# RWKV's sample step and first-half head norm placed ahead of the second half of the chunks, with nine buffers for cached keys and values

## The chip, the core and the metric

The kernel runs on one core of a Trainium2 chip. The metric is the device time of one execution in microseconds (us); lower is better. The names used for the engines are those of the profile: PE is the matrix engine (TensorE), PEld its weight loads, DVE the vector engine, ACT the scalar engine, POOL the GpSimd engine, SP the engine that issues most transfers.

## The reference, cut to what matters

One inference step of a two-layer hybrid decoder, for a prompt of 256 tokens and 8 sample rows (one token each) that share the weights. Each layer computes

```
proj = rmsnorm(x) @ w_in                       # one projection for four mixers
ya = moba_attend(q, k, v)                      # prompt: 256 own tokens
                                               # sample: top 3 of 8 cached blocks of 256 tokens, and the own token
yb = rglru_mixer(...)                          # convolution, gates, linear scan
yc = ssd_mixer(...)                            # prompt: 2 chunks of 128; sample: one recurrent step
yd = rwkv_mixer(...)                           # prompt: 256 steps; sample: one step
x = x + concat(ya, yb, yc, yd) @ w_out
x = x + cross_attn(rmsnorm(x), memory)
x = x + peer_ffn(rmsnorm(x))                   # product-key experts
```

In `rwkv_mixer`, y is the output of a recurrence over the tokens. It is normalised head by head (mean and variance over 64 columns), a bonus term sum(r*k*r_k)*v is added, and the sum is multiplied by a gate g. `k_past` and `v_past` of the sample rows are gathered from paged pools by a page table.

## The kernel before, in words

All activations lie feature-major: 128 partitions, then eight blocks of 128 features, then 264 columns (256 prompt tokens and 8 sample rows). A matmul against a float32 weight is made of three float32r matmuls: `load_w` splits a weight tile w into a rounded part wh (ACT) and the rest wl (DVE), and `proj` accumulates wh*hh, wh*hl and wl*hh over eight blocks, 24 matmuls into one PSUM tile `mm`. `inp(c, ...)` is such a projection with chunk c of w_in.

The program is one straight line of instructions. A scheduler puts each engine's instructions in an order from the order in which the source emits them, from their dependencies, from a modelled timeline and from the tiles that pools have free; so the place of a call in the source shifts the order on every engine without fixing it. Instructions of an engine, and the transfers that SP and POOL issue, go strictly in that order. `together()` keeps a group of matmuls adjacent.

The mixer part of a layer (`layer`, from line 464) goes in this order of emission:

- `moba_qk`: four projections and the rotation. Then the small `dt` product.
- `rwkv` is a generator and `next(rw)` runs it to its next `yield`. Its first piece makes seven projections, mixes each token with the one before, and forms decay, gate and the normalised key (a matmul `kn` for each of two head pairs). Its second piece is `rounds(0)`: two `unit`s (one for each head pair) go through the first 128 tokens as two chunks of 64. A unit makes scaled copies (`abd`, `kbd`), products `ob` and `m0`, then five rounds of `xl` and `xm` that invert a triangular matrix by doubling, with DVE's COPY_PREDICATED between them, and then `ob`, `ok`, `z` products, with the state `sl` at the end.
- `moba_sample`: for 8 rows, 16 groups of key pages. A group is four tiles `kvp` of [128, 2, 256], two loaded by SP (line 1221, two transfers of 128 KB each) and two gathered by POOL (line 1225, two indirect transfers each), and eight matmuls `asc` that read all four. So 16 groups need 64 gathers by POOL. After the scores come the selection of the blocks (`a2`, `a3` tiles) and 24 gathered value tiles `kvp` (line 1333), four to a group, with four matmuls `apv` each. All `kvp` tiles share `KVB` = 7 buffers; two more of them are taken by `ptm`, the probabilities, while values are gathered.
- `lru`: four projections and a scan. `ssd`: six projections, the convolution (`xb`), the step sizes (`dz`, `spd`), the decay products `rp`, the chunk products `fs`, `sc`, `y`, then the sample row's step (`t8s`, `sss`, `y16s`, a product `bk` from `bks`) and the norm (`yq`, `gm`, `sn`). Its large scratch tiles `sc1`, `sc2` have the tags `hh` and `hl`.
- `moba_prompt`: scores `as`, a softmax in `asm`, transposes `tp`, products `y`. `asm` and `apt` have the same tags `hh` and `hl`, so they take the buffers of `ssd`'s scratch when that is done.
- three more pieces of `rw`: `rounds(2)`, the two units for the last 128 tokens, which keep scratch in the weight pool's buffers (`unw`, `unwh`, `unwl`, `unz`); then the sample step `rwkv_sample` (`srt`, `srw`, DVE work on [128, 512], a product `bk` from `bkr`), the bonus and `finish(slice(0, 128))`, the head norm of the first 128 tokens; then `finish(slice(128, 264))`.
- products `mk` of the memory tokens, and the split of `ymix`; cross-attention (`w_out` first) follows.

`expand` lays out the sample step's operands through a tile `t8`, whose tag it shares with two tiles of `rwkv` (`up`, `pm`) in a pool with one buffer for that tag. `use(tag)` chooses the PSUM pool that the products in its block take.

Of the kernel before, what the change touches and what calls it, by code (L numbers as in the profile page):

```python
# [224 lines left out]
F32, F32R, F16, I32, U32, U8 = (getattr(mybir.dt, n) for n in ('float32', 'float32r', 'float16', 'int32', 'uint32', 'uint8'))  # L225
# [1 line left out]
OP = mybir.AluOpType  # L227
AX = mybir.AxisListType
EPS = 1e-6
KVB = 7  # L230
NF = 4
XT = 12
GS = 16384.0
# [10 lines left out]
def emit(tc, A, O, layers=(0, 1)):  # L244
# [223 lines left out]
    def layer(l, mx, v, following):  # L468
        me, mp, cm, vc, st = mx.es, mx.mp, mx.cm, mx.vc, mx.st
        st_h = st[:, 0:16].rearrange("p (c b) -> p c b", c=2)  # L470
        st_lc = st[:, 16:64].rearrange("p (c j b) -> p c j b", c=2, j=3)
        st_sc = st[:, 64:160].rearrange("p (c j b) -> p c j b", c=4, j=3)
        st_rs = st[:, 160:216].rearrange("p (c b) -> p c b", c=7)
        hp = me.enter_context(tc.tile_pool(name="h%d" % l, bufs=1, reuse_waits="tile"))
        eh = two(hp, ("eh", "el"), ("hh", "hl"))
        r = rstd(mp, v)
        for c in range(8):
            early(eh, vc('norm_mix'), c)
        if mx.pre is None:
            mx.prepare()  # L480
        pre = mx.pre
        win = A['w_in'][l]

        def inp(c, dst, half=False):

            o = proj(win[c], eh)
            if half:
                stt(dst, o, 0.5, r, OP.mult, OP.mult)
            else:
                tt(dst, o, r, OP.mult)  # L490
        with tc.tile_pool(name="z%d" % l, bufs=1, reuse_waits="tile") as zp:
            q, k = moba_qk(l, mp, cm, load_consts(zp, 'z'), inp)
        ymix = mp.tile([128, 8, NT], F32, name="ymix")

        rs = ExitStack()
        rp_ = rs.enter_context(tc.tile_pool(name="r%d" % l, bufs=1, reuse_waits="tile"))
        sp_ = rs.enter_context(tc.tile_pool(name="s%d" % l, bufs=1, reuse_waits="tile"))
        o = ps([4, NT], "dt")
        for c in range(8):
            for i, (a, b) in enumerate(((mx.dth, eh[0]), (mx.dth, eh[1]), (mx.dtl, eh[0]))):  # L500
                mm(o, a[:, c, :], b[:, c, :], start=c + i == 0, stop=c == 7 and i == 2)
        dtr = sp_.tile([4, NT], F32, name="dtr", tag="sn")
        tt(dtr, o, r[0:4], OP.mult)
        with use("pr"):
            rw = rwkv(l, mp, rp_, cm, vc, inp, pre, st_rs, ymix)
            next(rw)
        nc.gpsimd.dma_start(O['o_k'][l], k)
        v = moba_v(l, mp, inp)
        with use("pr"):
            next(rw)  # L510
        with use("pa"), tc.tile_pool(name="p%d" % l, bufs=1, side="right", reuse_waits="tile") as kp:
            moba_sample(l, mp, kp, cm, q, k, v, ymix, *mx.pages)
        xe = ExitStack()
        xk = xe.enter_context(tc.tile_pool(name="x%d" % l, bufs=1, side="right", reuse_waits="tile"))
        mem = xk.tile([128, 8, 256], F32, name="mem")
        mk = xk.tile([128, 8, 256], F32, name="mk")
        with tc.issue_after(wload[-1]):
            nc.sync.dma_start(mem, A['mem'])
        with use("ps"):
            lru(l, sp_, cm, vc, inp, pre, st_h, st_lc, ymix)  # L520
        with use("ps"):
            ssd(l, hp, sp_, cm, vc, inp, pre, dtr, st_sc, ymix)
        with use("ps"):
            moba_prompt(l, hp, sp_, cm, q, k, v, ymix)
        with use("mm"):
            next(rw)
        with use("ps"):
            next(rw)
        with use("pr"):
            next(rw)  # L530

        for c in range(NF):
            w = raw_w(A['x_wk'][l, c])
            o = ps([128, 256], "mk", "ps")
            for k in range(8):
                for j in (0, 128):
                    mm(o[:, j:j + 128], w[:, k, :], mem[:, k, j:j + 128], start=k + j == 0, stop=k == 7 and j > 0, skip=True)
            S.copy(mk[:, c, :], o)
        rs.close()
        yy = ExitStack()  # L540
        y = two(yy.enter_context(tc.tile_pool(name="y%d" % l, bufs=1, side="right", reuse_waits="tile")), ("yh", "yl"))
        for c in range(8):
            for w in (slice(0, 128), slice(128, NT)) if c > 5 else (slice(0, NT),):
                split(y[0][:, c, w], y[1][:, c, w], ymix[:, c, w])
        me.close()
        o = cross(l, vc, y, yy, mem, mk)
        r = peer(l, vc, *o, xe, following)
        return r

    def rwkv(l, bp_, mp, cm, vc, inp, pre, st_rs, ymix):  # L550
# [216 lines left out]
        def bonus():  # L767

            for c in range(2):
                t = mp.tile([128, NT], F32, name="kt", tag="t1", bufs=4)  # L770
                stt(t, R[:, c, :], vc('rwkv_r_k')[:, c:c + 1], k2[:, c, :], OP.mult, OP.mult)
                o = ps([128, NT], "gm")
                mm(o, cm['bones'], t)
                tt(ymix[:, 6 + c, :], W[:, c, :], o, OP.mult)
                stt(ymix[:, 6 + c, :], ymix[:, 6 + c, :], vc('rwkv_ln_b')[:, c:c + 1], gg[:, c, :], OP.add, OP.mult)
                act(gg[:, c, :], gg[:, c, :], AF.Copy, scale=vc('rwkv_ln_w')[:, c:c + 1])
# [18 lines left out]
        def rounds(n0):  # L795

            zz = wp.tile([128, 1024], F32, name="unz", tag="w", bufs=3) if n0 else None
            live = [unit(0, n0, zz), unit(1, n0, zz)]
            while live:
                live = [u for u in live if next(u, 0) is None]  # L800
        rounds(0)
        yield
        rounds(2)
        for c in range(2):
            for hl in range(2):
                q = slice(hl * 64, hl * 64 + 64)
                nc.gpsimd.dma_start(O['o_rwkv'][l, q, c, :], sl[q, c, q])
        yield

        with use("pr"):  # L810
            V.tensor_copy(yr[:, :, 256:264], rwkv_sample(l, mp, cm, lg, kk, bb, k2, R, W))
            bonus()
            finish(slice(0, 128))
        yield
        finish(slice(128, 264))
        yield
# [11 lines left out]
    def expand(l, mp, cm, q, nq, name):  # L828


        e = mp.tile([128, nq, 64], F32, name="e8" + name)
        for i0 in range(0, nq, 3):
            o = ps([128, 3, 64], "t8")
            for i in range(3):
                by_head(o[:, i, :], lambda c: q(i0 + i, c))
            t8 = mp.tile([128, 3, 64], F32, name="t8" + name, tag="t8")
            V.tensor_copy(t8, o)
            o = ps([128, 3, 64], "e8")
            mm(o.rearrange("p a b -> p (a b)"), cm['selx'], t8.rearrange("p a b -> p (a b)"))
            S.copy(e[:, i0:i0 + 3], o)  # L840
        return e
# [19 lines left out]
    def rwkv_sample(l, mp, cm, lg, kk, bb, k2, R, W):  # L861
        sp = mp.tile([128, 2, 2, 32], F32, name="sp")
        z = slice(232, 264)
        G.memset(sp[:, 0, :, 0:24], 0.0)
        act(sp[:, 0, :, 24:32], lg[:, :, 256:264], AF.Exp)
        ts(sp[:, 1], kk[:, :, z], -1.0)
        qs = (sp[:, 0], sp[:, 1], bb[:, :, z], k2[:, :, z], R[:, :, z], W[:, :, z])
        e = expand(l, mp, cm, lambda i, c: qs[i][:, c], 6, "r")
        v16 = part16(mp, cm, e[:, 5, :], "r")
        sa = mp.tile([128, 16], F32, name="sa")  # L870
        y16 = mp.tile([128, 16], F32, name="y16r")
        for i in range(2):
            r = slice(i * 8, i * 8 + 8)
            st = mp.tile([128, 8, 64], F32, name="srw")
            t = mp.tile([128, 8, 64], F32, name="srt")
            cols = slice(i * 512, i * 512 + 512)
            nc.sync.dma_start(st.rearrange("p a b -> p (a b)"), A['st_rwkv'][l, :, cols])

            def kb(j):
                return bc(e[:, j:j + 1, :], 128, 8, 64)  # L880

            def vb(a):
                return bc(a[:, r, None], 128, 8, 64)
            tt(t, st, kb(1), OP.mult)
            V.tensor_reduce(sa[:, r], t, axis=AX.X, op=OP.add)
            tt(st, st, kb(0), OP.mult)
            tt(t, kb(3), vb(v16), OP.mult)
            tt(st, st, t, OP.add)
            tt(t, kb(2), vb(sa), OP.mult)
            tt(st, st, t, OP.add)  # L890
            nc.gpsimd.dma_start(O['o_rwkvs'][l, :, cols], st.rearrange("p a b -> p (a b)"))
            tt(t, st, kb(4), OP.mult)
            V.tensor_reduce(y16[:, r], t, axis=AX.X, op=OP.add)
        return back(mp, cm, y16, "r")
# [974 lines left out]
```

## Time and profile before

| what | value |
|---|---|
| median of 3 runs | 2452.1 us (2447.89 to 2454.46) |
| profiled execution | 2452.99 us, its span 2451.2 us |
| PE busy | 2385.9 us of the span (97%) |
| DVE, ACT, POOL busy | 1758.8, 1367.6, 262.7 us |
| transfers | 480.63 MB, mean 196 GB/s |
| mixer part of layer 0 | 0 to about 242 us, then `mk` |
| mixer part of layer 1 | about 1227 to 1456 us, then `mk` |

A busy PE counts time in which a matmul was in the array. Where a page or an answer says "idle before", it is the time in which that engine had nothing, and what ended it. A stage of the program is read from its own stretch: the whole is bound by PE, but the mixer part of each layer is where PE is idle.

### The profile page before, as it was taken

How to read it: one execution, taken by the hardware profiler on the slowest of the kernel's cores; microseconds unless marked ns; L12 is line 12 of the kernel's file. 1: busy time of each engine (PE TensorE's matmuls, PEld its weight loads, DVE VectorE, ACT ScalarE, POOL GpSimd, SP SyncE). 2: the span in 40 equal slices, each digit the busy share in tenths (PEclk: the TensorE clock that was granted, in tenths of full speed). 3: DMA queues.
4: the chain of work that ended last, by engine and by line, in shares of the span. 5: the costliest groups of instructions: out<-in, count | busy, mean ns of one | idle time of the engine just before them, and what ended most of it. 6: DMA issues, size and time to landing. Idle time of an engine off the chain costs nothing.

```text
span 2451.2 us, 46818 instructions
## 1 busy us (share of the span) xinstructions
PE 2385.9 (97%) x17356; PEld 2135.8 (87%) x17356; DVE 1758.8 (72%) x3907; ACT 1367.6 (56%) x2794; POOL 262.7 (11%) x288
## 2 busy tenths in 40 slices
PE   9998999999999999999999989999999999999998
PEld 8776979999999988878887779899999999888886
DVE  6767677997698855555577577689967987555555
ACT  5434575555687744544554346655547876444444
POOL 5641000000000000000057300000000000000000
PEclk9999999999999999999999999999999999999999
DMA  8733775555675656665577338755556755556654
GB/s 283 230 112 102 261 308 200 172 180 177 202 241 183 194 175 189 190 207 188 189 243 221 105 102 300 276 196 175 174 180 215 225 190 181 187 187 187 188 188 137
DMA packets 146372, 480.63 MB, mean 196 GB/s; under 512 B 20288, under 2 KB 37728, under 8 KB 141024
## 3 DMA queue, kind: packets, MB, share of 16 engines
q1 hardware_dynamic: 129088, 423.46, 52.9%
q0 software_dynamic: 17056, 54.17, 7.4%
q8 instruction: 137, 2.24, 0.4%
q14 instruction: 91, 0.75, 0.1%
HBM read 468.53 MB, written 9.03 MB: 195 GB/s over the span
## 4 chain that ended last, share of the span: by engine, by line
PE 88%; DMA 5%; ACT 2%; DVE 2%; issue 1%; SPq 0%; POOL 0%; DVEq 0%; ACTq 0%; POOLq 0%
PE mm L288 42%; PE pv L288 29%; PE g L288 2%; DMA kvp<-in_kc 2%; PE mv L288 2%; PE asc L288 2%; PE xm L288 1%; PE mk L288 1%; PE xo L288 1%; PE sc L288 1%; DMA kvp<-in_vc,vidx 1%; PE var L288 1%; DMA w<-in_ud 1%; PE xl L288 1%; PE z L288 1%
## 5 line engine op out<-in xcount | busy, mean ns | idle before, releaser
L298 DVE TENSOR_TENSOR wl<-w,wh 128x1024 fp32r<-128x1024 f32 x662 | 808.1, 1222 | 432.3 <-ACT wh L313 427.8
L313 ACT CAST wh<-w 128x1024 fp32r<-128x1024 f32 x662 | 694.5, 1050 | 756.6 <-PE pv L288 358.3
L288 PE MATMUL mm<-hh,wh 128*128 128x256 f32 (+1 forms) x2176 | 545.9, 288 | 2.4 <-ACT HG L310 2.4
L288 PE MATMUL mm<-hl,wh 128*128 128x256 f32 (+1 forms) x2176 | 536.3, 284 | 0.0
L288 PE MATMUL pv<-wh,ghl 128*128 128x512 f32 x2048 | 524.6, 396 | 0.2 <-ACT ghl L313 0.2
L288 PEld LDWEIGHTS pv<-wh,ghl 128*128 128x128 f32 x2048 | 385.7, 188 | 91.9 <-ACT ghl L313 0.6
L288 PEld LDWEIGHTS mm<-hh,wh 128*128 128x128 f32 x2176 | 410.5, 189 | 3.8 <-ACT HG L310 3.2
L288 PEld LDWEIGHTS mm<-hl,wh 128*128 128x128 f32 x2176 | 410.7, 189 | 3.3 <-issue 3.3
L288 PE MATMUL mm<-hh,wl 128*128 128x256 f32 (+1 forms) x2176 | 300.6, 282 | 0.0
L288 PE MATMUL pv<-wl,ghl 128*128 128x512 f32 x1024 | 283.8, 396 | 0.6 <-DVE wl L298 0.6
L288 PEld LDWEIGHTS mm<-hh,wl 128*128 128x128 f32 x2176 | 276.5, 189 | 0.4 <-issue 0.4
L288 PEld LDWEIGHTS pv<-wl,ghl 128*128 128x128 f32 x1024 | 192.8, 188 | 46.6 <-DVE wl L298 1.2
L310 ACT ACTIVATE gb<-ga,ewt 128x128 f16<-128x128 f16 x512 | 173.2, 433 | 21.1 <-DVE ga L298 17.2
L1225 POOL DMA_INDIRECT kvp<-in_kc,pidx x128 | 140.3, 1096 | 233.9 <-ACT eh L310 179.0
L288 PE MATMUL mm<-eh,wh 128*128 128x264 f32 x624 | 162.2, 294 | 0.0
L288 PE MATMUL mm<-el,wh 128*128 128x264 f32 x624 | 160.7, 291 | 0.0
L288 PEld LDWEIGHTS mm<-eh,wh 128*128 128x128 f32 x624 | 118.1, 190 | 6.0 <-issue 4.1
L288 PEld LDWEIGHTS mm<-el,wh 128*128 128x128 f32 x624 | 118.4, 190 | 3.0 <-issue 2.1
L298 DVE TENSOR_TENSOR ghl<-HG,ghl 128x256 fp32r<-128x256 f32 x256 | 107.1, 419 | 0.0
L313 ACT CAST ghl<-HG 128x256 fp32r<-128x256 f32 x256 | 101.7, 398 | 2.4 <-DVE HG L298 2.4
L298 DVE TENSOR_TENSOR HG<-HG,g 128x256 f32<-128x256 f32 (+31 forms) x254 | 86.7, 349 | 16.4 <-PE g L288 15.9
L288 PE MATMUL mm<-eh,wl 128*128 128x264 f32 x624 | 93.3, 289 | 0.0
(674 smaller groups left out, 3280.0 us busy)
## 6 DMA issues: line engine op xcount, KB each, us to landing
w<-in_ud SPq DMA_DIRECT2D x256, 512.0 KB
w<-in_vd SPq DMA_DIRECT2D x256, 512.0 KB
w<-in_w_in SPq DMA_DIRECT2D x46, 512.0 KB
kvp<-in_kc SPq DMA_DIRECT2D x128, 128.0 KB
xkt<-in_mk SPq DMA_DIRECT2D x16, 1024.0 KB
xkt<-in_mv SPq DMA_DIRECT2D x16, 1024.0 KB
w<-in_peer_wq SPq DMA_DIRECT2D x32, 512.0 KB
w<-in_x_wk SPq DMA_DIRECT2D x16, 512.0 KB
```

What stands on the lines that cost most here:

```text
L288: T.matmul(out, lhsT, rhs, start=start, stop=stop, skip_group_check=skip)
L298: (eng or V).tensor_tensor(out, a, b, op=op)
L310: S.activation(out, a, f, **kw)
L313: S.copy(h, x)
L1225: nc.gpsimd.indirect_dma_start(out=t[:, j, :], out_offset=None, in_=A['kc'].rearrange("l n p f -> (l n p) f"), in_offset=bass.IndirectOffs ...
```

## The change

In `rwkv` the piece with `rwkv_sample`, `bonus` and `finish(slice(0, 128))` moves ahead of `rounds(2)`, so it becomes the third piece instead of the fourth. In `layer` that piece is now taken before `moba_prompt`, with PSUM tag `pr`, and `rounds(2)` after it, with `mm` as before. `expand`'s tile `t8` gets a buffer of its own instead of the shared tag. `KVB` goes from 7 to 9. No operation is added or removed.

```diff
--- before.py
+++ after.py
@@ -227,7 +227,7 @@
 OP = mybir.AluOpType
 AX = mybir.AxisListType
 EPS = 1e-6
-KVB = 7
+KVB = 9
 NF = 4
 XT = 12
 GS = 16384.0
@@ -520,11 +520,11 @@
             lru(l, sp_, cm, vc, inp, pre, st_h, st_lc, ymix)
         with use("ps"):
             ssd(l, hp, sp_, cm, vc, inp, pre, dtr, st_sc, ymix)
+        with use("pr"):
+            next(rw)
         with use("ps"):
             moba_prompt(l, hp, sp_, cm, q, k, v, ymix)
         with use("mm"):
-            next(rw)
-        with use("ps"):
             next(rw)
         with use("pr"):
             next(rw)
@@ -800,18 +800,17 @@
                 live = [u for u in live if next(u, 0) is None]
         rounds(0)
         yield
+
+        V.tensor_copy(yr[:, :, 256:264], rwkv_sample(l, mp, cm, lg, kk, bb, k2, R, W))
+        bonus()
+        finish(slice(0, 128))
+        yield
         rounds(2)
         for c in range(2):
             for hl in range(2):
                 q = slice(hl * 64, hl * 64 + 64)
                 nc.gpsimd.dma_start(O['o_rwkv'][l, q, c, :], sl[q, c, q])
         yield
-
-        with use("pr"):
-            V.tensor_copy(yr[:, :, 256:264], rwkv_sample(l, mp, cm, lg, kk, bb, k2, R, W))
-            bonus()
-            finish(slice(0, 128))
-        yield
         finish(slice(128, 264))
         yield
 
@@ -833,7 +832,7 @@
             o = ps([128, 3, 64], "t8")
             for i in range(3):
                 by_head(o[:, i, :], lambda c: q(i0 + i, c))
-            t8 = mp.tile([128, 3, 64], F32, name="t8" + name, tag="t8")
+            t8 = mp.tile([128, 3, 64], F32, name="t8" + name)
             V.tensor_copy(t8, o)
             o = ps([128, 3, 64], "e8")
             mm(o.rearrange("p a b -> p (a b)"), cm['selx'], t8.rearrange("p a b -> p (a b)"))
```

Lines behind the moved block are one less in the new numbering. What the scheduler makes of it is told at three places of layer 1, in PE's order. A row is a line, an operation, the tile written and the tiles read, the shape of the result, and how many alike follow each other.

The first place is in the key gather, near the two `kn` products of `rwkv`. Before, around the eighth group of key products `asc`, the next but one behind the first `kn`:

```order
L288 MATMUL mm<-el,wh 128x264
L288 MATMUL mm<-eh,wl 128x264 x4
L288 MATMUL asc<-kvp,aqz 32x256 x8
L288 MATMUL mm<-eh,wl 128x264 x4
L288 MATMUL mm<-eh,wh 128x264
L288 MATMUL mm<-el,wh 128x264
```

Now, from the first `kn` on (`a` is a small product of `moba_sample`, `m` with a number is `m0`):

```order
L288 MATMUL kn<-kt,cst_m 128x264
L288 MATMUL asc<-kvp,aqz 32x256 x8
L288 MATMUL kn<-kt,cst_m 128x264
L288 MATMUL asc<-kvp,aqz 32x256 x16
L288 MATMUL ob<-abd,kbd 128x256 x4
L288 MATMUL asc<-kvp,aqz 32x256 x8
L288 MATMUL m_15501<-kbd,abd 128x128
L681 MATMUL m_15501<-cst_g,abd 128x128
```

Before, projections `mm` stand between all groups of `asc` there. Now from the first `kn` to the `xm` products of the first units no `mm` stands at all: six groups of `asc` (48 instructions) have only two `kn`, four `ob`, eight `m0`, eight `xl`, twelve `xm` and four `ok` among them. Of the 422 `mm` products that stood between the first and the last `asc` of this layer, 231 are left; the other 191 now stand between the last `asc` and the last `apv`. On SP's queue 40 loads of `kvp` now follow each other in this layer with no load of w_in among them, where no more than six did until its last w_in load.

The second place is the value gather of layer 1, at the third of the six `apv` groups in both kernels. Before:

```order
L288 MATMUL xl<-unwl 128x128 x2
L288 MATMUL z<-ss,qp 128x128 x2
L288 MATMUL sc<-xb 128x256
L288 MATMUL sc<-xb 128x128
L288 MATMUL apv<-kvp 32x512 x4
L288 MATMUL y<-sc_17239,sc_17240 64x256
L288 MATMUL xm<-unwh,xl 128x128
```

Now:

```order
L288 MATMUL mm<-eh,wl 128x264 x4
L288 MATMUL apv<-kvp 32x512 x4
L288 MATMUL z<-wt,br 128x128
L288 MATMUL z<-kv 128x128
L288 MATMUL z<-wt,br 128x128
L288 MATMUL z<-kv 128x128
L288 MATMUL z<-ss,qp 128x128
L288 MATMUL mm<-eh,wl 128x264 x4
L288 MATMUL mm<-eh,wh 128x264
L288 MATMUL mm<-el,wh 128x264
```

Before, `ssd`'s products `sc` and `y` and the units of `rounds(2)` (`xl` from `unwl`, `xm`) stand here. Now projections stand here, and `ssd`'s products and the units come behind the last `apv`.

The third place is the end of layer 1's mixer, from `ssd`'s sample product (`bk` from `bks`) on. Before:

```order
L288 MATMUL bk<-cst_m,bks 128x8 x2
L288 MATMUL xl<-unwl 128x128 x4
L288 MATMUL xm<-unwh,xl 128x128 x4
L288 MATMUL ob<-unz,unwh 128x256 x4
L288 MATMUL ok<-unwl,unwh 128x256 x2
L288 MATMUL gm<-yq,cst_m 128x264 x2
L288 MATMUL as<-ak,aq 128x128
L288 MATMUL as<-ak,aq 128x256
L288 MATMUL ok<-unwl,unwh 128x256 x2
```

Now:

```order
L288 MATMUL bk<-cst_m,bks 128x8 x2
L288 MATMUL gm<-kt,cst_m 128x272
L288 MATMUL gm<-yq,cst_m 128x264 x2
L288 MATMUL as<-ak,aq 128x128
L288 MATMUL as<-ak,aq 128x256
L288 MATMUL as<-ak,aq 128x128
L288 MATMUL as<-ak,aq 128x256
```

Before, the units' last products `xl`, `xm`, `ob`, `ok` and `z` stand between `bk` and the transposes `tp` of `moba_prompt`. Now all of them stand ahead of `bk`; behind it come three `gm`, eight `as`, sixteen `tp` and eight `y`, and then `mk`. In layer 0 projections are left between nearly all groups of `asc`, and units still stand beside `moba_prompt`'s end.

## Rows read from the trace of the kernel before

**Rows 1.** Page, part 1: busy us, share of the span, instructions.

```profile
PE 2385.9 (97%) x17356; PEld 2135.8 (87%) x17356; DVE 1758.8 (72%) x3907; ACT 1367.6 (56%) x2794; POOL 262.7 (11%) x288
```

**Rows 2.** Windows, layer 1 first: us; PE, PEld, DVE, ACT, POOL busy; clock, DMA, GB/s.

```profile
1250.99:1353.20 102.21, 95.98 (x799) 80.92 (x798) 74.11 (x182) 49.12 (x82) 71.47 (x70) 0.97 0.77 236
1353.20:1416.60 63.40, 59.26 (x556) 45.91 (x554) 33.70 (x112) 21.61 (x68) 23.86 (x26) 0.96 0.39 110
1416.60:1456.00 39.40, 31.74 (x195) 25.49 (x191) 31.84 (x71) 21.17 (x57) 3.30 (x6) 0.94 0.26 89
34.90:138.60 103.70, 96.30 (x806) 81.59 (x805) 75.26 (x181) 50.26 (x84) 69.35 (x70) 0.98 0.76 237
138.60:201.80 63.20, 58.53 (x559) 45.89 (x560) 34.53 (x115) 21.14 (x67) 24.86 (x26) 0.98 0.39 110
201.80:242.00 40.20, 33.48 (x195) 27.14 (x193) 32.42 (x70) 21.77 (x58) 3.30 (x6) 0.90 0.25 87
```

**Rows 3.** Waits of PE in layer 1, then in layer 0: us, times, longest.

```profile
PE asc L288 <- DMA kvp<-in_kc: 5.4, 4, 2.2
PE apv L288 <- DMA kvp<-in_vc,vidx: 4.1, 2, 2.1
...
PE asc L288 <- DMA kvp<-in_kc: 6.1, 7, 2.2
PE apv L288 <- DMA kvp<-in_vc,vidx: 4.7, 2, 4.4
```

**Rows 4.** Chain of waits, layer 1: start us, us, engine, tile, records.

```profile
1258.26 5.29 PE mm L288 x42
1263.55 1.00 PE asc L288 x16
1290.51 0.45 PE kn L288 x2
1331.02 1.09 PE xm L288 x8
1375.56 1.06 PE ob L288 x4
```

**Rows 5.** POOL's key gathers: tile `kvp` from 85 us, waits and transfers of layer 1.

```profile
L1225 POOL DMA_INDIRECT kvp<-in_kc,pidx x28: 942/947/1982, 85.3 to 132.2; - x28
...
DMA to landing us min/median/max: 2.8/3.4/3.9
...
POOL kvp L1225 <- issue: 13.4, 45, 0.3
...
kvp<-in_kc,pidx POOLq DMA_INDIRECT x56, 3.9
```

**Rows 6.** End of layer 1's mixer, timeline by engine, and its busy time.

```profile
1430.56 1.80 DVE L423 RECIPROCAL sn<-sn 128x264 f32<-128x264 f32 x1 [0.87 <-ACT sn L310]
1438.45 0.28 DVE L307 SCALAR_TENSOR_TENSOR asm<-as,cst_m 128x128 f32<-128x128 f32 x1
1441.70 1.22 DVE L1147 TENSOR_REDUCE amx<-asm 128x4 f32<-128x1024 f32 x1
...
1422.66 0.61 PE L288 MATMUL bk<-cst_m,bks 128*128 128x8 f32 x4
1429.72 0.92 PE L288 MATMUL as<-ak,aq 64*128 64x128 f32 x4
1447.61 1.40 PE L1161 MATMUL tp<-cst_g,asm 128*128 128x128 f32 x6
1453.84 2.22 PE L288 MATMUL y<-apt,avt 128*64 128x256 f32 x16 [1.50 <-ACT avt L1168]
1455.99 1.16 PE L288 MATMUL mk<-mem,w 128*128 128x128 f32 x8
...
1422.66:1456.00 33.34, 26.22 (x155) 20.48 (x151) 27.08 (x63) 19.32 (x51) 3.30 (x6) 0.95 0.22 74
```

**Rows 7.** Ten us of layer 1's key gather; the sixth number is the granted clock.

```profile
1280.00:1290.00 10.00, 7.76 (x57) 6.62 (x56) 6.85 (x20) 3.48 (x6) 3.63 (x5) 0.83 0.92 225
```

## The prediction, as it was made before the run

> **What bounds the kernel now.** I read the busy time of the whole first: PE is in use for 97% of the span [rows 1], so a change that adds no operation can only move the 65 us in which PE has nothing. Next I read the busy time by stage [rows 2], to see where in a mixer that idle time lies. In layer 1 the key gather has 102.21 us with 95.98 busy (6.2 idle), the value gather 63.40 with 59.26 (4.1 idle), the rest up to `mk` 39.40 with 31.74 (7.7 idle). Layer 0 has 7.4, 4.7 and 6.7. Third come the waits that PE had [rows 3]: in the gathers most of the idle time ends with a landing `kvp`, four stalls of 5.4 us in all for keys and two of 4.1 us for values in layer 1, 6.1 and 4.7 in layer 0. Fourth, the chain of waits [rows 4] shows what fills PE in the key gather: stretches of `mm` between groups of `asc`, so that gathers land behind projections. That cover is what this change touches.
>
> A price for each product comes from these rows and the timeline [rows 4, 6]. There xN counts records, and a float32 product leaves two: an `mm` 5.29/42 = 0.126 us, a group of eight `asc` 1.00, `kn` 0.45, `xm` 1.09/4 = 0.27, `ob` 1.06/2 = 0.53, `gm` the same as `ob` for want of a row.
>
> **The change part by part.** The sum is made against the profiled execution, 2452.99 us, which is 0.9 us (0.04%) above the median.
>
> *The source moves three pieces; PE's work stays.* No operation comes or goes, so PE's busy time is unchanged but for the clock, and every term below is idle time of PE. `t8`'s own buffer only lets the moved step start; I cost it at nothing, since the DVE work it releases lies beside projections.
>
> *Key gather of layer 1: +11.2 us.* With nine buffers the scheduler lets `asc` come sooner, and 191 `mm` (191 x 0.126 = 24.1 us) go behind the last `asc`. Six groups then follow each other with this work only: 6 x 1.00, two `kn` 0.9, four `ob` and four `ok` 8 x 0.53 = 4.2, and `m0`, `xl`, `xm`, 28 at 0.27 = 7.6 (the first two priced as `xm`): 18.7 us. Each group needs four gathers by POOL, 24 in all. A gather takes 0.947 us and up to 0.3 us of issue behind it, so 1.247 us, and 24 take 29.9 us [rows 5]. PE is short of work for 29.9 - 18.7 = 11.2 us. The earlier stalls of rows 3 I leave as they are. Low end: nine buffers hold two whole groups, so if both have landed at the start, 16 gathers (20.0 us) and a last landing of 3.4 us leave 23.4 - 18.7 = +4.7. High end: the pitch of the whole stage with POOL's waits in it, 102.21/64 = 1.60 us, so 38.3 - 18.7 = +19.6. I take the pitch of POOL's own rows, since by its order nothing else stands in its queue there.
>
> *Value gather of layer 1: -2 us (-4.1 to 0).* It gains the 24.1 us of projections, which wait for no value tile, and loses as much of `ssd` and of the second units to the tail. Half of its 4.1 us of stalls should be covered. POOL's queue now holds the outputs of `lru` and `ssd` and two pairs of MEMSETs between value gathers; a gather behind one of them waits for it, and that is why I don't take all.
>
> *Tail of layer 1, behind `ssd`'s `bk`: +7.3 us.* `moba_prompt` needs the buffers of `ssd`'s scratch. Before, the units' products lay beside this chain: 33.34 us from `bk` to `mk` with 26.22 busy, 7.1 idle [rows 6]. Now the units are done by then, and the chain is left with `bk` 0.6, three `gm` 1.6, eight `as` 4 x 0.92 = 3.7, sixteen `tp` 16 x 1.40/6 = 3.7 and eight `y` 2.2: 11.8 us of work. The chain itself is 9.7 us from `bk` (1422.66) to the end of the norm's RECIPROCAL (1432.36), eight masks `asm` of 0.28 = 2.2, and 14.3 us from the last maximum (1441.70) to `mk` (1455.99): 26.2 us, so 14.4 us idle, 7.3 more than before. Low end: DVE is free of the sample step and 4 us drop out of the last piece, +3.3. High end: the whole 33.34 us stay, 21.5 idle, +14.4. What is late next is `mk` and with it `w_out`, because the split of `ymix` waits for `moba_prompt`.
>
> *Tail ahead of that `bk`: +5 us.* The tail's 31.74 us and the 24.1 that come in make 55.8; less the 11.8 behind `bk`, 44 us of `ssd` and unit products stand between the last `apv` and `bk`, without projections as filler. The nearest rows are the whole tail, 7.66 of 39.40 idle (19%), and its part up to `bk`, 39.40 - 33.34 = 6.06 us with 31.74 - 26.22 = 5.52 busy (9% idle) [rows 2, 6]. 44 us of work at 9% brings 4.4 us and at 19% 10.3; the 0.5 that was idle there goes off, so +3.8 to +9.8. I take +5, near the lower, as two units and two chunks of `ssd` interleave.
>
> *Clock: +2 us (0 to +5).* Around a pause before, 2.2 us of idle in ten, the granted clock is 0.83 [rows 7]. [...] New pauses of this kind come in the key gather and the tail; I take about one such loss, and three for the end of the range. [...]
>
> *Layer 0: -2 us (-10.8 to +3).* Here projections are left between nearly all groups of `asc` and units still stand beside `moba_prompt`. Two more buffers should take a third of the 6.1 us of key stalls; all stalls of rows 3 for this layer are 10.8 us, the low end. The high end is a tail that is stretched a little, by the low end of layer 1's.
>
> Sum: 11.2 - 2 + 7.3 + 5 + 2 - 2 = +21.5, so **2474.5 us**. All low ends together: 4.7 - 4.1 + 3.3 + 3.8 + 0 - 10.8 = -3.1, 2450. All high: 19.6 + 0 + 14.4 + 9.8 + 5 + 3 = +51.8, 2505.
>
> **The rivals.** *A: the buffers carry it, faster.* PE's stalls on `kvp` are 5.4 + 4.1 + 6.1 + 4.7 = 20.3 us [rows 3], while POOL is in use for only 71.47 of the key gather's 102.21 us [rows 2], so it has room. If the nine buffers keep two groups ahead, all of these stalls go, and only the tail's low ends of 3.3 and 3.8 are paid: 2453 - 20.3 + 7.1, about 2440. It decides at a pitch of 18.7/16 = 1.17 us a gather, with two groups landed at the start. Against it stands POOL's 1.247, and that the landing adds 3.4. [...]
>
> *B: most of it is paid back, no change or a little slower.* The key burst costs its low end, the tail its low ends, and the value stalls and half of layer 0's go: 4.7 + 3.3 + 3.8 - 4.1 - 5.4 = +2.3, some 2455, with 2450 to 2463 about it (the tail's terms as I took them give 5.2 more). For it: POOL is ahead by two groups when the burst begins. Against it: the order leaves no filler in the tail.
>
> *C: both chains keep their length of today.* The pitch stays 1.60 us, as the buffers, and not POOL, set it, and `bk` to `mk` stays at 33 us: 8.4 + 7.1 on top of the forecast, 2490.
>
> *D: nothing happens that PE feels*, because the pieces stand in PE's order where stalls cover them: 2451 to 2455. The order of layer 1 is against it.
>
> **How the numbers follow.** Forecast 0.55, A 0.10, B 0.20, C 0.12, D 0.03. A measurement of this kernel can tell about 0.3%, here 7.4 us, from no change. A is faster, 0.10; D and half of B are the same, 0.13; the forecast, C and the other half of B are slower, 0.77. The range leaves out A and the upper part of C and of the high ends: 2450 to 2498.
>
> **What would show it.** In the changed kernel's trace of layer 1: PE idle between the first `kn` and the first units' `xm`, about 11 us, ended by `kvp` of the key gather, with POOL's gathers at a pitch near 1.25 us; at 1.6, C. The value gather has the projections of `lru` and `ssd` and no long wait for `apv`. From `bks`' product to the first `mk` 26 us with 12 busy; near 33, C; near 22, B. `rounds(2)` is over ahead of `bk`. Layer 0's three stages are within 3 us of before. The forecast is wrong if the key burst has under 5 us of idle, or if the tail's chain runs beside work that I counted ahead of it.

## The result, and the profile after

The changed kernel takes 2482.59 us (median of 5 runs, 2477.71 to 2482.66), against 2452.1 us before: a ratio of 1.012, interval 1.0108 to 1.0131. So it is 30.5 us slower. The forecast was 2474.5 us with a range of 2450 to 2498.

The busy time of the whole comes first, part 1 of the page of the changed kernel.

```profile
span 2480.8 us, 46790 instructions
PE 2403.0 (97%) x17356; PEld 2134.8 (86%) x17356; DVE 1759.2 (71%) x3907; ACT 1372.0 (55%) x2795; POOL 260.1 (10%) x288
```

The span grew by 29.6 us. PE's idle time grew from 65.3 us [rows 1] to 77.8, by 12.5 us, and PE's busy time by 17.1 us with the same 17356 instructions. The forecast had put nearly everything on the idle side. Next is the busy time by stage of the changed kernel: stretch, its length, then PE, PEld, DVE, ACT and POOL busy, the granted clock, the DMA share and GB/s. Layer 0 is in three stages (key gather, value gather, the rest up to `mk`) and the stretch up to layer 1 is one row. Then come layer 1's key gather, value gather, tail up to `ssd`'s `bk`, and tail from there to `mk`.

```profile
33.65:124.85 91.20, 86.60 (x698) 66.71 (x697) 56.14 (x129) 42.93 (x73) 64.65 (x63) 0.98 0.83 262
124.85:193.82 68.97, 65.98 (x543) 52.74 (x543) 44.95 (x149) 28.06 (x78) 28.26 (x31) 0.95 0.34 101
193.82:246.88 53.06, 43.70 (x314) 35.42 (x314) 42.36 (x95) 25.05 (x66) 3.79 (x7) 0.94 0.22 77
246.90:1255.17 1008.27, 1001.18 (x7128) 909.82 (x7127) 736.75 (x1587) 590.15 (x1188) 35.03 (x43) 1.00 0.63 204
1255.17:1339.00 83.83, 72.73 (x595) 54.30 (x594) 43.83 (x98) 28.47 (x50) 56.03 (x58) 0.98 0.78 245
1339.00:1405.20 66.20, 61.92 (x554) 51.54 (x551) 45.23 (x122) 33.07 (x69) 32.79 (x33) 0.95 0.48 136
1405.20:1457.17 51.97, 45.97 (x344) 38.17 (x341) 42.87 (x124) 18.92 (x51) 4.37 (x8) 1.00 0.16 54
1457.17:1487.21 30.04, 16.18 (x60) 10.42 (x59) 11.05 (x22) 13.17 (x38) 0.00 (x0) 0.55 0.13 47
```

From the first `asc` to `mk` layer 1 takes 232.04 us, where before it took 205.08 (1250.92 to 1456.00). That is 27.0 of the 29.6 us. PE is idle for 11.1 + 4.3 + 6.0 + 13.9 = 35.2 us in these four rows, against 18.0 before, so 17.2 us more. PE's busy time there is 196.8 us against 187.05, 9.75 more for the same products. Layer 0 reached `mk` 4.9 us later. There, too, work moved from the key gather to the end: its stages are 12.5 us shorter, 5.8 longer and 12.9 longer than before [rows 2]. Between the layers almost nothing changed (1008.27 us against 1008.92).

What a stage waits for is in the waits of PE in layer 1 of the changed kernel: us, times, longest.

```profile
PE asc L288 <- DMA kvp<-in_kc: 8.0, 5, 2.3
PE tp L1160 <- ACT asm L310: 6.7, 1, 6.7
PE gm L288 <- ACT yq L310: 3.8, 1, 3.8
PE asc L288 <- DMA kvp<-in_kc,pidx: 2.5, 2, 1.8
PE apv L288 <- DMA kvp<-in_vc,vidx: 0.8, 2, 0.5
```

`kvp<-in_kc` with `pidx` is a gather by POOL, without it a load by SP. The stall for value tiles went, from 4.1 us to 0.8 [rows 3]. The stall for keys did not: 8.0 and 2.5 us, against 5.4 and 0.8 before (the 0.8, for POOL's gathers, is not in [rows 3]). The second and third row are new and stand in `moba_prompt`'s chain and in the norm of `ssd` ahead of it.

The burst itself is one stretch, from the first `kn` to the first units' `xm`: the stage row, three of POOL's gathers in it, in the timeline of POOL, and two waits of PE, in the timeline of PE.

```profile
1295.80:1321.50 25.70, 16.74 (x125) 10.20 (x125) 14.90 (x39) 4.90 (x10) 19.91 (x21) 0.98 0.78 240
...
1311.94 0.94 POOL L1224 DMA_INDIRECT kvp<-in_kc,pidx  x1 [0.30 <-issue]
1313.19 0.95 POOL L1224 DMA_INDIRECT kvp<-in_kc,pidx  x1 [0.30 <-issue]
1314.44 0.95 POOL L1224 DMA_INDIRECT kvp<-in_kc,pidx  x1 [0.30 <-DMA kvp<-in_kc,pidx]
...
1300.22 0.59 PE L288 MATMUL asc<-kvp,aqz 128*32 128x256 f32 x2 [2.32 <-DMA kvp<-in_kc]
1305.39 1.25 PE L288 MATMUL asc<-kvp,aqz 128*32 128x256 f32 x14 [0.66 <-DMA kvp<-in_kc,pidx]
```

POOL starts most gathers 1.25 us apart, with no pause over 0.30 us, and PE has 16.7 us of work in 25.7 us, 9.0 idle. POOL has no pause that more buffers could fill. But it is not shown that PE waits for POOL's pace. PE's five waits for `kvp<-in_kc`, 8.0 us in all, stand in this stretch, each in front of the first products of a group, and they end with a load by SP; one of 0.66 us ends with a gather by POOL. SP's queue waited for buffers too: from 1290 to 1325 us it waited four times, 4.3 us in all, for `asc` products. So PE waits for the transfers of both queues, and which of them sets the pace no run tells.

Last, the chain of waits in the tail behind `bk`, 1457 to 1487 us: start, us, engine, tile.

```profile
1457.82 0.74 PE gm L288 x2
1459.10 1.85 DVE kn L423
1461.61 0.65 ACT yq L310
1462.31 2.14 PE gm L288 x4
1465.05 1.80 DVE sn L423
...
1468.25 1.66 PE as L288 x6
1471.38 1.28 ACT L310
1473.37 2.93 ACT asm L310 x13
1476.56 2.87 ACT asm L310 x8
1479.85 1.54 PE tp L1160 x6
1481.39 1.06 PE tp L1166 x4
1483.12 4.16 PE y L288 x16
```

It is one chain through PE, ACT and DVE in turn. PE's links are long: the `y` products take 4.16 us where they took 2.22 before, and four records of `gm` 2.14 us where they took 1.05:

```profile
1428.74 1.05 PE L288 MATMUL gm<-yq,cst_m 128*128 128x264 f32 x4
```

The granted clock of this stretch is 0.55 of full speed.

### The profile page after: what moved, and what is told of

Its sections match the earlier page's. It is cut to its first block, busy times and chain, and to the rows that moved or that the text cites. A ratio compares the mean times of both kernels' runs of the same rounds, so it can differ in the third digit from the quotient of the medians.

```text
span 2480.8 us, 46790 instructions
## 1 busy us (share of the span) xinstructions
PE 2403.0 (97%) x17356; PEld 2134.8 (86%) x17356; DVE 1759.2 (71%) x3907; ACT 1372.0 (55%) x2795; POOL 260.1 (10%) x288
## 4 chain that ended last, share of the span: by engine, by line
PE 87%; DVE 4%; ACT 3%; DMA 3%; issue 1%; POOL 1%; SPq 0%; DVEq 0%; ACTq 0%; POOLq 0%
PE mm L288 43%; PE pv L288 28%; PE g L288 3%; PE mv L288 2%; PE mk L288 1%; PE asc L288 1%; DMA kvp<-in_kc 1%; PE xo L288 1%; PE xm L288 1%; DMA kvp<-in_kc,pidx 1%; PE sc L288 1%; PE var L288 1%; ACT wh L313 1%; PE z L288 1%; PE xp L288 1%
## 5 line engine op out<-in xcount | busy, mean ns | idle before, releaser
L310 ACT ACTIVATE gb<-ga,ewt 128x128 f16<-128x128 f16 x512 | 173.1, 433 | 22.1 <-DVE ga L298 17.2
L1224 POOL DMA_INDIRECT kvp<-in_kc,pidx x128 | 134.7, 1052 | 48.5 <-issue 29.7
## 6 DMA issues: line engine op xcount, KB each, us to landing
xkt<-in_mv SPq DMA_DIRECT2D x16, 1024.0 KB, 10.8
```

The lines of the kernel that those rows point to most:

```text
L310: S.activation(out, a, f, **kw)
L1224: nc.gpsimd.indirect_dma_start(out=t[:, j, :], out_offset=None, in_=A['kc'].rearrange("l n p f -> (l n p) f"), in_offset=bass.IndirectOffs ...
```

## The experiments

Each ratio is against the kernel before on the same chip. Four kernels ran on each chip. On the first of them the kernel before took 2468.86 us, on the others 2449.22 and 2450.6, so times are compared within one chip.

### The two halves of the change apart

**Nine buffers alone.** The kernel before with

```diff
-KVB = 7
+KVB = 9
```

> The kernel before with nine buffers for cached keys and values, the pieces of RWKV and t8's tag left where they were. Theory (the buffers alone reorder the work): PE's order has the same burst of key groups as the changed kernel, layer 1's stages are those of the changed kernel within 3 us, ssd comes late, and the time is 2477 to 2484 us. Rival (the moved pieces uncover the tail): the tail keeps its units beside moba_prompt, and the time is 2440 to 2455 us.

Measured: 2512.18 us, ratio 1.0174 (1.0152 to 1.0197). **Moved pieces alone**, with `t8` in a buffer of its own:

```diff
-KVB = 9
+KVB = 7
```

> The changed kernel with seven buffers: pieces moved, t8 in a buffer of its own. Theory (the buffers alone reorder the work): key and value gather as in the kernel before, tail of layer 1 38 to 42 us against 39.4, time 2449 to 2456 us. Rival (the moved pieces uncover the tail): from the bks product to mk 30 us with PE at half clock, time 2465 to 2480 us.

Measured: 2474.11 us, ratio 1.0016 (1.0005 to 1.0027). Both are above the stated times, and this chip is slower for the kernel before too. As ratios, the move alone is at the upper end of what the theory said, and nine buffers alone lost more than it said (1.0174, where 2477 to 2484 us would be 1.010 to 1.013). Both ratios are on the side of the theory: the buffers carry the loss, the moved pieces almost none. Layer 1's stages of the two, key gather first, show it: nine buffers alone in four rows, the move alone in three.

```profile
1264.13:1363.94 99.81, 81.08 (x593) 56.47 (x592) 42.38 (x96) 27.99 (x49) 57.80 (x58) 0.88 0.64 206
1363.94:1437.65 73.71, 66.63 (x559) 54.82 (x559) 48.40 (x126) 33.79 (x69) 31.13 (x33) 0.91 0.41 123
1437.65:1487.13 49.48, 44.65 (x334) 37.23 (x333) 41.66 (x119) 18.95 (x51) 3.42 (x7) 1.00 0.16 54
1487.13:1514.92 27.79, 14.91 (x61) 9.41 (x61) 11.40 (x23) 13.07 (x38) 0.96 (x2) 0.65 0.16 56
```

```profile
1274.03:1375.83 101.80, 94.70 (x799) 80.56 (x799) 72.88 (x179) 48.77 (x81) 72.50 (x69) 1.00 0.75 233
1375.83:1445.23 69.40, 63.13 (x560) 49.88 (x559) 33.84 (x114) 22.62 (x70) 23.92 (x26) 0.90 0.34 99
1445.23:1483.56 38.33, 33.89 (x187) 26.00 (x186) 31.76 (x71) 21.40 (x56) 3.24 (x6) 0.91 0.27 95
```

With nine buffers the key gather holds 593 products instead of 799 in nearly the same time, and those that left it stand in the last two rows: 395 products in 77.3 us, where the move alone has 187 in 38.3 us. Against the expectation, the stage lengths are not those of the changed kernel within 3 us: the key gather is 99.81 us here and 83.83 there, on another chip (on the chip of the next experiment nine buffers alone take 82.63).

**The changed kernel and nine buffers alone, side by side.** What the moved pieces do when the buffers are nine was asked on a third chip, with both kernels unchanged.

> The changed kernel beside nine buffers alone on one chip, to size the moved pieces. Theory (the moved pieces give a little back when the buffers are nine): 1.010 to 1.015, and 2 to 8 us less than the next. Rival (the moved pieces make no difference): within 2 us of the next.

> The kernel before with nine buffers alone, on the same chip as the run before it. Theory: 1.011 to 1.018, 2 to 8 us more than the changed kernel. Rival: within 2 us of it.

Measured: 2480.27 us, ratio 1.0121 (1.0106 to 1.0136), and 2473.89 us, ratio 1.0099 (1.0084 to 1.0113). Theory and rival are both wrong. The moved pieces give nothing back; they cost 6.4 us, with four runs of each, all of the one above all of the other. A part of that shows in one profile of each: from `bks`' product to `mk` 27.74 us with nine buffers alone and 30.57 with the change. There PE waits 1.1 us for `yq` in the first, and 3.8 us in the second. A RECIPROCAL of `finish` (`kn`) stands in both tails, but `yq` is made from the product of `ymix` and `zz`. With nine buffers alone DVE has that product ahead of the RECIPROCAL, with the change behind it (the last two rows, from the first profile of the changed kernel).

```profile
1451.78 0.70 DVE L298 TENSOR_TENSOR ymix<-ymix,zz 128x528 f32<-128x528 f32 x1
1452.70 1.85 DVE L423 RECIPROCAL kn<-kn 128x272 f32<-128x272 f32 x1 [0.22 <-ACT kn L310]
...
1459.10 1.85 DVE L423 RECIPROCAL kn<-kn 128x272 f32<-128x272 f32 x1
1460.87 0.64 DVE L298 TENSOR_TENSOR ymix<-ymix,zz 128x528 f32<-128x528 f32 x1
```

The rest was not traced to a place.

### Is it the burst, or nine buffers as such

**Key products without raised priority, in both layers.** `together` also raises the priority of its products, by an offset of 2000. Here it takes the offset as an argument, and the call around the `asc` products passes 0.

```diff
-                with together():
+                with together(0):
```

> The changed kernel, nine buffers, but the key products asc have no raised priority, so the scheduler may not put them ahead of projections that were emitted before them. Theory (it is the burst, not the buffers as such): ssd's sample product is early again and units stand beside moba_prompt, layer 1's mixer from the first asc to mk is under 215 us against 232, the time is 2450 to 2466 us. Rival (nine buffers cost by themselves, through transfers that collide): the time stays at 2475 us or above.

Measured: 2507.28 us, ratio 1.015 (1.0129 to 1.0171). Layer 1's order did what the theory said: `bks`' product came 2.3 us behind the last `apv`, where nine buffers alone have 49.5, and first `asc` to `mk` took 202.7 us. That figure flatters, since without priority the first `asc` itself stands later, 1033.3 us behind layer 0's `mk` instead of 1007.7. From layer 0's `mk` to layer 1's `mk` the kernel takes 1236.0 us, against 1258.5 with nine buffers alone and 1222.6 with the move alone on that chip. And the time stayed where the rival had it. Layer 0 had become longer: `mk` started at 278.3 us, against 256.4 with nine buffers alone and 261.0 with the move alone. This edit changed both layers, so the total can't decide between theory and rival, and it was split.

**The same in layer 1 alone.**

```diff
-                with together():
+                with together(0 if l else 2000):
```

> The changed kernel, with the raised priority of the key products kept in layer 0 and taken away in layer 1. Theory (layer 1's burst is what costs, nine buffers are harmless): layer 0 as in the changed kernel, from layer 0's mk to layer 1's mk 15 to 25 us less than there, time 2455 to 2470 us where the changed kernel has 2482. Rival (nine buffers cost by themselves): within 6 us of the changed kernel.

Measured: 2453.27 us, ratio 1.0013 (1.0 to 1.0026); it had been expected at 2455 to 2470. Layer 0 keeps its order of the changed kernel, nine buffers are still there, and the loss is gone. From layer 0's `mk` to layer 1's `mk` it takes 1216.15 us. The changed kernel on the same chip, with the kernel before for a profile, gives the other side:

> The changed kernel once more on this chip. Theory (buffers reorder the work, the moved pieces give a little back): 1.010 to 1.016 of the time before, less than the 1.0174 of nine buffers alone. Rival (the moved pieces cost too): 1.0174 or more.

> The kernel before once more, for a profile from the same chip as the next runs. Both theories: layer 1 from the first asc to mk 203 to 212 us, with 16 to 20 us of it idle on PE.

Measured: the changed kernel 2479.03 us, ratio 1.012 (1.0102 to 1.0139), the stretch from `mk` to `mk` 1238.07 us; the kernel before 2453.18 us, the stretch 1215.06 us. The ratio of 1.012 is in the range of the theory that the moved pieces give a little back, but that theory compares two chips; on one chip, above, they cost. From the first `asc` to `mk` the kernel before has 205.98 us with 20.9 idle, above the 20 that was expected at most. The key gathers of this pair, the kernel before first:

```profile
1250.83:1356.02 105.19, 95.30 (x799) 81.16 (x799) 74.29 (x182) 49.08 (x82) 72.01 (x70) 0.97 0.75 230
1244.54:1327.93 83.39, 74.56 (x595) 54.40 (x594) 43.91 (x98) 28.52 (x50) 55.89 (x58) 0.94 0.78 246
```

PE is idle for 9.9 us in the first and 8.8 in the second. So in this pair the key gather has no more idle time with the burst than without; what came in stands in the tail, 7.0 us idle before and 21.7 now. Layer 1's stages without raised priority:

```profile
1276.14:1368.47 92.33, 83.08 (x659) 62.74 (x658) 63.26 (x168) 38.21 (x62) 64.08 (x64) 0.98 0.63 201
1368.47:1424.51 56.04, 52.22 (x515) 40.28 (x516) 41.31 (x114) 20.67 (x65) 27.52 (x29) 1.00 0.50 148
1424.51:1460.55 36.04, 30.81 (x179) 25.05 (x177) 25.44 (x59) 20.99 (x55) 2.71 (x5) 0.91 0.21 74
```

The tail from `bks`' product has 30.81 us of work in 36.04 us: units stand beside `moba_prompt` again. So nine buffers are harmless in layer 1 when the order does not follow them.

**Nine buffers in layer 0, seven in layer 1.** Each of the three tiles named `kvp` has

```diff
-bufs=KVB
+bufs=(7 if l else 9)
```

> The changed kernel with nine buffers in layer 0 and seven in layer 1. Theory (the loss is layer 1's burst): from layer 0's mk to layer 1's mk 1210 to 1222 us, as with seven buffers, against 1238 to 1240 of the changed kernel; time 0.995 to 1.005 of before. Rival (layer 0 loses as well): 1.006 or more.

Measured: 2452.31 us, ratio 1.0011 (0.9999 to 1.0023), from `mk` to `mk` 1216.6 us. Beside the changed kernel on this chip (2480.27 us) that is 28.0 us for two buffers in one layer; the edit before gave 25.8 us on its chip. The two edits that take the burst away, by priority and by buffers, agree, and the theory holds: the loss is that of layer 1's order. They take away the burst and the bare tail together, so they don't size the two apart.

### The clock in the tail

**Products in the pauses.** The changed kernel, in layer 1 alone, with products whose result nobody reads, and one small copy on DVE that starts the first six:

```diff
+        V.tensor_copy(dd, ys[:, :, 256:264])
+        for i in range(6):
+            mm(d[:, 0:256], cm['bones'], bc(dd.rearrange("p a b -> p (a b)")[:, :, None], 128, 16, 16))
...
         V.tensor_reduce(mx[:, 1, :], sm[:, :, 128:384], axis=AX.X, op=OP.max, negate=True)
+        for i in range(10):
+            mm(d[:, 0:256], cm['bones'], bc(mx.rearrange("p a b -> p (a b)")[:, :, None], 128, 8, 32))
```

> The changed kernel with sixteen products more in layer 1's tail whose result nobody reads: six 128x256 behind ssd's sample product, ten behind the maximum of moba_prompt's scores, where PE has nothing to do. Read from bks' product to mk alone, since the order of later stages shifts too. Theory (PE's pauses drop its clock, and the half clock lengthens the chain): granted clock there over 0.75 instead of 0.55, sixteen y products 2.2 to 3.0 us instead of 4.2, the stretch 25 to 28 us instead of 30 although work was added. Rival (the chain is DVE's and ACT's, the clock costs nothing): the stretch stays at 30 us or grows by the added products.

Measured: from `bks`' product to `mk` 28.35 us at a granted clock of 0.76, against 30.04 at 0.55. Two rows each divide the stretch at the first `tp`, the changed kernel first, and its timeline row of the `y` products follows for the kernel with added products.

```profile
1457.17:1477.02 19.85, 7.72 (x28) 4.88 (x27) 11.05 (x22) 8.47 (x27) 0.00 (x0) 0.58 0.19 71
1477.02:1487.21 10.19, 8.46 (x33) 5.54 (x33) 0.00 (x0) 4.70 (x12) 0.00 (x0) 0.50 0.01 2
```

```profile
1454.93:1477.62 22.69, 17.14 (x60) 12.80 (x60) 11.13 (x23) 10.80 (x33) 0.00 (x0) 0.70 0.15 56
1477.62:1483.28 5.66, 4.56 (x34) 3.25 (x32) 0.00 (x0) 2.31 (x5) 0.00 (x0) 1.00 0.01 3
```

```profile
1481.12 2.22 PE L288 MATMUL y<-apt,avt 128*64 128x256 f32 x16 [0.68 <-ACT avt L1176]
```

The changed kernel has 30.04 us and `y` products of 4.16 us on this chip too. Behind the first `tp` the same products take 5.66 us at a granted clock of 1.00 and 10.19 at 0.50. Of the 4.5 us between them 3.9 are PE's busy time (4.56 against 8.46), the rest is shorter pauses. The added products themselves delayed the first `tp` by 2.8 us, which is why the whole gained only 1.7. The theory holds on the clock and on `y`; the stretch is shorter, as it said, but above its 28 us. The row at 1.00 follows 7.28 us of added products without a pause; in the row at 0.50 PE is busy for 8.46 of 10.19 us.

### Eight buffers

> The kernel before with eight buffers instead of seven or nine. Its order of PE has 383 of 422 projections left between the key groups of layer 1, and 91 products between the bks product and mk. Theory (the loss comes with the size of the burst): no loss, the stalls on kvp get less, 2440 to 2453 us. Rival (each further buffer moves the same way): half of the loss, 2462 to 2470 us.

The edit is `KVB = 8` in the kernel before. Measured on the first chip: 2475.62 us, ratio 1.0024 (1.0012 to 1.0036). That is far from half of the loss, so the loss doesn't grow evenly with each buffer, but there is no gain either: it is 0.24% slower, and as a ratio above the theory's 2440 to 2453 us. In its profile layer 0 reached `mk` at 253.0 us, where the move alone had 261.0, and layer 1 took 215.3 us to its `mk`, against 209.5. That asked for eight in layer 0 and seven in layer 1:

```diff
-bufs=KVB
+bufs=(7 if l else 8)
```

> The kernel before with eight buffers in layer 0 and seven in layer 1, pieces not moved: the mildest form of the change's gain, a layer 0 with fewer stalls on kvp and no burst in layer 1. Theory: layer 0 up to mk 2 to 8 us shorter than with seven, 0.996 to 1.000 of before. Rival (stalls in layer 0 come back at its value gather or tail): 1.000 to 1.004.

Measured: 2443.0 us, ratio 0.9967 (0.9955 to 0.9979), faster than both kernels: 7.6 us less than before, 37.3 less than the changed kernel on that chip. Layer 0 reaches `mk` at 233.38 us (before 241.96 and 241.75), with these stages:

```profile
34.10:131.80 97.70, 89.68 (x752) 72.15 (x751) 65.98 (x151) 44.87 (x73) 71.29 (x69) 1.00 0.76 246
131.80:191.14 59.34, 58.39 (x515) 45.99 (x515) 36.20 (x130) 25.12 (x73) 24.25 (x26) 1.00 0.41 118
191.14:233.38 42.24, 37.73 (x288) 29.98 (x287) 36.89 (x83) 23.10 (x62) 3.83 (x7) 1.00 0.28 95
```

Its value gather has 1.0 us idle where there were 4.7 [rows 2], and the granted clock is 1.00 in all three stages where it was 0.98, 0.98 and 0.90. Not all that this profile gained is layer 0's: from `mk` to `mk` it takes 1209.8 us, with seven buffers as in the kernel before, which takes 1214.0 and 1215.1; and it is the fastest of the six runs.

## Why the prediction was right, and where it was off

The sign, the place and the range held; the sum was +21.5 us and the result +30.5. By its own steps, against the profiled execution:

- **Key gather of layer 1, forecast +11.2 us.** Idle time went from 6.2 to 11.1 us, +4.9; in the second pair of profiles from 9.9 to 8.8. The step that failed is to leave the earlier stalls as they were: the burst's idle time in large part took their place instead of coming on top. Outside the burst 2.1 us are left of 6.2. In the burst the idle time is of the forecast size, 9.0 us up to the first `xm`, but the reason given is not shown to be the one. The forecast's six groups reach up to the next `mm`, 1295.80 to 1328.72: 32.9 us with 23.6 busy, for 29.9 and 18.7 forecast. Length and work were both put too low, by 3.0 and 4.9 us, so it is in part luck that their difference, 9.3 us, comes near the 11.2. And the forecast priced POOL's gathers alone, while SP's loads ended nearly all of the waits; the waits for keys in [rows 3] had been for SP's loads already.
- **Value gather, forecast -2 us.** The stall on values fell by 3.3 us, as argued, but other pauses came and the idle time stayed (4.3 for 4.1).
- **Tail behind `bk`, forecast 14.4 us of idle in 26.2.** It is 13.9 in 30.04. The first piece, `bk` to the end of the norm's RECIPROCAL, was 9.7 us as forecast (1457.17 to 1466.85), but by luck: it has the RECIPROCAL of `finish` in it, which did not stand there before, and with nine buffers alone, where `yq` does not wait for it, the piece takes 7.8. The excess is PE's part: 16.2 us busy for 11.8, at a clock of 0.55.
- **Tail ahead of `bk`, forecast +5 us.** 6.0 us idle with 46.0 busy, for 44 of work at 9%; the 0.5 us from before goes off, so +5.5.
- **Clock, forecast +2 us (0 to +5), and PE's work unchanged but for it.** PE's busy time in layer 1 rose by 9.75 us (and by 10.0 in the second pair of profiles). The rise over the forecast's price is 4.4 us behind `bk` (16.2 for 11.8), and the run with added products shows 3.9 us of busy time for the clock there. This part of the term was mis-sized: the prediction took one pause of the size in [rows 7] as its measure; but in this tail the clock stayed low from one pause to the next, so nearly the whole chain ran at half clock and not the first products behind a pause: the granted clock is 0.79 from 1457.17 to the end of the wait for `yq` at 1462.31, and 0.50 from there to `mk`, 24.90 us with 14.95 busy. The 2 us was the author's estimate from [rows 7], where 0.17 of ten us is 1.7; no run shows what one such pause costs, and what the runs showed in its place is those 3.9 us. The other 5 us lie in the stages ahead of `bk`, and they are not the clock's: its granted share is 0.98, 0.95 and 1.00 there, and before it was 0.97, 0.96 and, for the whole tail, 0.94 [rows 2]. So the step that left PE's work unchanged but for the clock failed. The same products were busy for longer where they stand apart: two records of `asc` behind a wait take 0.59 us, and sixteen in a row took 1.00 [rows 4]. That this makes up the 5 us is not shown.
- **Layer 0, forecast -2 us (-10.8 to +3).** +4.9 in the profile that was compared, outside the bounds. But this order of layer 0 was profiled six times, and reached `mk` at 246.88, 236.67, 244.15, 244.08, 244.40 and 244.32 us (before: 241.96 and 241.75). The middle of these is 2.4 us later than before: inside the bounds, and on the other side of nothing than forecast. The sign that its stages would be within 3 us of before failed.

Some of the errors cancel: the key gather was put 6.3 us too high, and PE's busy time 7.75 too low. That the sum comes as near as 9 us is in part luck.

Rival A, the buffers carry it, did not happen: the stalls on values went, those on keys did not. The order put the groups closer together as soon as the scheduler's model had more buffers, but that this is why the key stalls stayed is not shown: without raised priority in layer 1, nine buffers still left 6.5 us of them. Rival B gave 2455 and C 2490; the result lies between the forecast and C. But C's first mechanism, gathers at a pitch of 1.60 us, was not there; its second, a tail of 33 us, was half there, at 30.04.

The forecast argued from the order that the buffers were the cause and the moved pieces had little part. The runs show the first (25.8 and 28.0 us in layer 1, by two edits). Of the second they show a small cost, 0.16% with seven buffers and 6.4 us with nine, where the prediction had none.

## What to carry to other kernels

Where a scheduler orders the work, a pool's depth is an input to the order: two more buffers made it bring raised-priority products forward into a burst in which PE was idle for 9.0 of 25.7 us, and the filler that had covered the end of the mixer was spent. Compare the order before and after, count what is left beside each chain, and try the depth layer by layer: eight in one layer gained 0.33%, nine in the other lost over 1%. Price a chain that will be left alone with PE's products at half clock from its first pause on, as in this tail (granted clock 0.50 from 1462.31 to `mk`, the `y` products 4.16 us for 2.22), and products that will stand apart at more than they take in a row (here two records of `asc` 0.59 us behind a wait, sixteen in a row 1.00).

## What had not been expected of the hardware

In this tail the half clock did not end with a pause: in the changed kernel the granted clock was 0.50 for the last 10.19 us, although PE was busy for 8.46 of them. Added products that are of no use made the stretch shorter by 1.7 us (28.35 for 30.04). And chips differ: the kernel before took 2468.86 us on one and 2449.22 on another, and on the slower one nine buffers cost more (1.0174 against 1.0099).
